# A hybrid encoder block in float32r pairs: the gate stores move to ScalarE's queue, and ScalarE's order in the early feed-forward is written by hand

## The chip, the cores and the metric

One core of a Trainium2 chip runs the whole block. The metric is the device time of one launch in microseconds (us), the median of several runs. Engines: TensorE (PE, with its weight loads PEld), VectorE (DVE), ScalarE (ACT), GpSimd (POOL), and SyncE (SP), which here only issues transfers.

## The reference, cut to what matters

```python
h = concat([meta(16), x(1024)])                     # D = 1024
n = rms_norm(h)
qa, ka, va, qb, kb, vb, ga, gb = split(n @ w_in)
y_a = differential_attention(qa, ka, va)            # 4 heads, two softmaxes each, all keys
y_b = windowed_gqa(qb, kb, vb, sink)                # 8 heads, window 128, sinks
h += (sigmoid(ga) * (y_a @ w_ba) + sigmoid(gb) * (y_b @ w_bb)) @ w_o
f = rms_norm(h)
h += (silu(f @ w_gate) * (f @ w_up)) @ w_down       # D_FF = 2816
out = rms_norm(h)[:, 16:]
```

Everything is float32 at the borders.

## The kernel before, in words

**Precision.** Each factor of a matmul is a pair: a high part (the value rounded to float32r, made by a ScalarE copy, L117 and others) and a low part (the rest, made by a subtraction on VectorE or GpSimd, L118). A product is three matmuls: high by high, high by low, low by high.

**Products of blocks.** The gate projections and the feed-forward are cut into 2 x 2 blocks and computed with seven products instead of eight, numbered 1 to 7, on sums and differences of blocks. Products of one output accumulate in the same PSUM bank: 1, 6, 7 and 4 in one, 2 in another, 5 and 3 in a third. There are eight banks.

**The attention stage** (about 322 to 620 us). A loop over 4 heads x 8 blocks of 128 tokens computes scores (L814), VectorE adds the distance bias and takes the minimum (L817), ScalarE takes the exponential (L824), VectorE combines the two maps (L837), and the block before is transposed (L849) and multiplied with the values (L862). Between these steps `fill` draws single steps from `gate_steps`, the generator of the gate products: a step is three matmuls (L751), and four steps end a product. At the end of products 2, 5, 3 and 4, ScalarE copies the bank into a buffer `gate_stage` (two of them, L759). At the end of 1, 6 and 7, VectorE adds the bank to a buffer `gk` that was loaded from memory (L756). In both cases the result is stored to memory with L760, issued by SyncE; there are 26 stores from `gate_stage` and 24 from `gk`. The next stage loads these results again.

**What sets the order.** TensorE's order is that of the program throughout these stages. The other engines' instructions, and the transfers on SyncE's queue, are ordered by a planner that simulates the program, unless a `manual_schedule` block names the engine: then its instructions keep the program's order. In the first attention block that holds for ScalarE and VectorE.

**The early feed-forward** (about 770 to 836 us). The out projection writes `h` in 128-token blocks; `norm_f` normalises a block (ScalarE's square on L1237), and `turn_f` transposes it into two banks. For blocks 4 to 7, `turn_f` forms sums with the kept halves of blocks 0 to 3 (L1268 to L1274): L1268 and L1272 read the first bank, L1269, L1270 (a ScalarE copy), L1271 (ScalarE, high part) and L1273 the second, so both banks come free when all of these have run, and L1272 needs L1270 first. Block 4 is turned before the loop. The sums are split into pairs for products 6, 5, 7 and 4 by `split_t`: four ScalarE copies (L1321) for each block, GpSimd's low parts for product 4 (L1323), and VectorE's low parts for the others put off to `low_of` (L1325).

The loop over `nf` products (`product_f`, L1347) starts before all blocks are there: for the first three pairs of weight columns (`N_EARLY`) products 1 and 2 come first, since they need only blocks 0 to 3. That is 12 products, with the turns of blocks 5, 6 and 7 ahead of products 0, 2 and 4. `prepare(limit)` makes the weight pairs ahead of use, as many as fit `limit` slots (eight by default): it loads raw weights, forms sums on VectorE for products 6 and 3 (L1163 to L1169), and splits with one ScalarE copy (L117) and one GpSimd subtraction (L118). ScalarE also copies a bank after products 1, 5 and 6 (L1372, L1375) and applies Silu after 2, 7, 3 and 4 (L1358). Before the change only VectorE's order is by hand in products 0 to 11.

Of the kernel before, what the change touches and what calls it, by code (L numbers as in the profile page):

```python
# [9 lines left out]
F32 = mybir.dt.float32  # L10
# [3 lines left out]
AF = mybir.ActivationFunctionType  # L14
# [5 lines left out]
P = 128  # L20
# [53 lines left out]
def encoder_block(ctx: ExitStack, tc: tile.TileContext, x, meta, norm_mix, w_in, lq1, lk1, lq2, lk2,  # L74
                  subln, sink, w_ba, w_bb, w_o, norm_ffn, w_g, w_u, w_d, norm_final, out, dbg=None):
    nc = tc.nc
# [5 lines left out]
    def f32(ap):  # L82
        return ap.bitcast(F32)

    def pool(name, side="left", space=None, bufs=1):
        kw = {} if space is None else {"space": space}
        if space is not DRAM:
            kw["reuse_waits"] = "tile"
        cm = tc.tile_pool(name=name, bufs=bufs, side=side, **kw)
        p = cm.__enter__()  # L90
        return p, lambda: cm.__exit__(None, None, None)

    const, close_const = pool("const")
    small, close_small = pool("small", bufs=4)
# [21 lines left out]
    def split(hi, lo, src, lo_eng):  # L116
        nc.scalar.activation(hi, src, AF.Copy)  # L117
        lo_eng.tensor_tensor(lo, src, f32(hi), ALU.subtract)  # L118
# [41 lines left out]
    def pp_bank(name):  # L160
        return bank(psum1, "pp", name, 3 if psum1 is not psum2 else PP2)
# [304 lines left out]
    for i in range(2):  # L466
        cols = slice(960 * i, 960 * i + 960)
# [37 lines left out]
    def quad(hl, kh, half):  # L505
        return (hT_hi, hT_lo)[hl][:, 4 * kh:4 * kh + 4, half * 512:half * 512 + 512]
# [70 lines left out]
    def load_sums(p, kh, half):  # L577
        for hl in range(2):
            nc.sync.dma_start(f32(quad(hl, kh, half)), ts_d[p][:, hl])
# [35 lines left out]
    def g_place(p, k):  # L615
        row, half = G_OUT[p]
        return g_d[2 * k + row][:, half * 512:half * 512 + 512]
# [23 lines left out]
    def g_ahead(n):  # L641
        for i, (what, far) in enumerate(((g_load, GR_BUFS - 1), (g_split, GO_BUFS - 1))):
            while g_done[i] < min(n + far, len(order_g)):
                if i and held_back is not None:
                    held_back.append(g_done[i])
                else:
                    what(g_done[i])
                g_done[i] += 1
# [74 lines left out]
    for k in range(0, 6, 2):  # L723
        ensure(1)
        wh, wl = prepped.pop((k, k + 1))
        for i in range(2):
# [4 lines left out]
            st = f32(stage.tile([P, 2, 512], F32R, tag="qk", name="gate_first", bufs=QK_BUFS))[:, 0]  # L731
# [10 lines left out]
    def gate_steps():  # L742
        for n, (p, k) in enumerate(order_g):
            g_ahead(n + 1)
            op, act = g_ready.pop((p, k)), G_ACT[p]
            if p in (2, 5, 1):
                g_bank[k] = pp_bank(f"pg{p}_{k}")
            ps = g_bank[k]
            for c in range(4):
                for i, (a, b) in enumerate(((0, 0), (0, 1), (1, 0))):  # L750
                    nc.tensor.matmul(ps, op[:, a, c], quad(b, *act)[:, c], start=(p in (2, 5, 1) and c == 0 and i == 0),  # L751
                                     stop=(p in (2, 3, 4) and c == 3 and i == 2), skip_group_check=True)
                if c == 3:
                    if p in (1, 6, 7):
                        st = g_kept.pop((p, k))
                        nc.vector.tensor_tensor(st, ps, st, ALU.add)  # L756
                    else:
                        st = gpool.tile([P, 512], F32, tag="g", name="gate_stage", bufs=G_BUFS)
                        nc.scalar.copy(st, ps)  # L759
                    nc.sync.dma_start(g_place(p, k), st)  # L760
                    if (p, k) in ((5, 3), (5, 7), (3, 7)):
                        later_p = {(5, 3): 6, (5, 7): 7, (3, 7): 4}[p, k]
                        load_sums(later_p, *G_ACT[later_p])
                yield

    gates = gate_steps()
    close_psum1()
    close_tpool()
# [15 lines left out]
    def branch_w(p, o, src, nme, raw=None):  # L784
        if raw is None:
            raw = raw_tile(f"wbr{nme}_{o}")[:, 0:512]
            load_w(raw, o, src)
        w = raw.rearrange("p (c n) -> p c n", n=P)
        wh = p.tile([P, 2, 4, P], F32R, tag="wh", name=f"wbh{nme}_{o}", bufs=WB_BUFS)
        split(wh[:, 0], wh[:, 1], w, nc.vector if nme == "a" and o >= 4 else nc.gpsimd)  # L790
        return wh
# [208 lines left out]
    def op_tile(name):  # L1000
        return ring.tile([P, 2, 512], F32R, tag="op", name=name, bufs=OP_BUFS)

    def raw_tile(name):
        return ring.tile([P, 1024], F32, tag="raw", name=name, bufs=RING_RAW)
# [3 lines left out]
    def prep_wo(q, c):  # L1008
        w = raw_tile(f"wo_{q}_{c}")[:, 0:512]
        nc.sync.dma_start(w, w_o[c * P:(c + 1) * P, q * 512:q * 512 + 512])  # L1010
        wos[q, c] = op_tile(f"woh_{q}_{c}")
        split(wos[q, c][:, 0], wos[q, c][:, 1], w, nc.gpsimd)
# [4 lines left out]
    for h in range(2):  # L1017
        cols = slice(h * 512, h * 512 + 512)
# [22 lines left out]
    def gated(i, o, half, w, src):  # L1041
        tk = slice(half * 512, half * 512 + 512)
        gt = ypool.tile([P, 512], F32, tag="gt", name=f"gt_{i}_{o}_{half}", bufs=GT_BUFS)
        nc.sync.dma_start(gt, g_d[8 * i + o][:, tk])
        nc.scalar.activation(gt, gt, AF.Sigmoid)
        ps = ps_bank(f"ppa_{o}_{half}_{i}")
        branch_mm(ps, w, src, tk)
        return gt, ps, tk
# [3 lines left out]
    for o in range(DC):  # L1052
        w = first_w[o] if o < 2 else branch_w(ypool, o, w_bb, "b")
        for half in range(2):
            gt, ps, tk = gated(0, o, half, w, yb)
# [16 lines left out]
    for n, (o, half) in enumerate(order_a):  # L1072
        if o not in ws_a:
            ws_a[o] = branch_w(ypool, o, w_ba, "a")
        gt, ps, tk = gated(1, o, half, ws_a[o], ya)
        nc.vector.tensor_tensor(gt, gt, ps, ALU.mult)
        nc.gpsimd.tensor_tensor(gt, gt, tb_row(o, tk), ALU.add)
        split(mT[:, o, 0, tk], mT[:, o, 1, tk], gt, nc.vector)
        if n >= 8:
            prep_wo(0, n - 8)  # L1080
    close_ya()
    close_ya0()
    close_ypool()
# [37 lines left out]
    ops, prepared, used, loaded, freed = {}, [0], [0], [0], [0]  # L1121

    def prepare(limit=OP_BUFS):
        while prepared[0] < len(steps):
            kind, s = steps[prepared[0]]
            need = 1 if kind == "f" else 2
            if used[0] + need > limit or (kind == "d" and prepared[0] >= nf + loaded[0]):
                break
            used[0] += need
            ops[kind, s] = weights(s[2], s[0], s[1]) if kind == "f" else ops_pm(*s)  # L1130
            prepared[0] += 1
        while prepared[0] >= nf and loaded[0] < min(len(steps) - nf, freed[0] + RING_RAW):
            load_d(*steps[nf + loaded[0]][1])
            loaded[0] += 1
# [177 lines left out]
    def c_tile(name):  # L1312
        return cpools[0].tile([P, 512], F32, tag="c", name=name, bufs=C_BUFS) if cpools else p_tile(name)

    lows = {p: [] for p in (6, 5, 7)}

    def split_t(u):
        cols = slice(u * P, u * P + P)
        for p in (6, 5, 7, 4):
            hi, lo, t = t_ops[p][:, 0, :, cols], t_ops[p][:, 1, :, cols], sums_t[u][p]  # L1320
            nc.scalar.activation(hi, t, AF.Copy)  # L1321
            if p == 4:
                nc.gpsimd.tensor_tensor(lo, t, f32(hi), ALU.subtract)  # L1323
            else:
                lows[p].append(lambda hi=hi, lo=lo, t=t: nc.vector.tensor_tensor(lo, t, f32(hi), ALU.subtract))  # L1325

    def low_of(n):
        for p in (6, 5, 7):
            while n > 0 and lows[p]:
                lows[p].pop(0)()  # L1330
                n -= 1

    st = {}
# [64 lines left out]
                nc.sync.dma_start(a_d[3][fp], s4)  # L1398

    AFTER = {0: 5, 2: 6, 4: 7}  # L1400
    for n in range(nf):
        if n not in range(5, 8):
            prepare()
        if n == 0:
            order_dve = tc.manual_schedule(engines={mybir.EngineType.DVE})
            order_dve.__enter__()
        if n in AFTER:
            turn_f(AFTER[n])
            if n == 0:
                split_t(0)  # L1410
            split_t(AFTER[n] - 4)
        product_f(*steps[n][1])
        used[0] -= 1
        if n in (1, 2, 3, 4):
            low_of({1: 1, 2: 1, 3: 1, 4: 1}[n])
        if n == 5:
            prepare(used[0] + 1)
            mults.pop(0)()
            low_of(1)
        if n == 7:  # L1420
            prepare()
            low_of(2)
            mults.pop(0)()
        if n == 9:
            low_of(9)
        if n == 11:
            while mults:
                mults.pop(0)()
            order_dve.__exit__(None, None, None)
            close_h2()  # L1430
            cp, close_cpool = pool("cpool")
            cpools.append(cp)
# [85 lines left out]
    for n in range(nf, len(steps)):  # L1518
        p, j = steps[n][1]
# [3 lines left out]
        if p in LOADS:  # L1523
            at, half, col = LOADS[p]
            if at <= j < at + 4:
                t, cols = 4 * half + j - at, slice(col * 512, col * 512 + 512)
# [60 lines left out]
```

## Time and profile before

| | us |
|---|---|
| median of 3 runs | 1440.44 |
| the runs | 1440.28, 1440.44, 1446.15 |
| the profiled execution | 1441.88 |
| its span, first to last instruction | 1440.0 |
| TensorE busy in the span | 1420.1 |
| ScalarE, VectorE, GpSimd busy | 680.1, 899.8, 643.6 |

The profile lists what each engine did and when. Waits are put down to the instruction or transfer that came last. A group's row gives the line, engine, operation, output <- inputs, shapes and count, then busy time and mean length of one, then the idle time just before, with what ended it. "SPq" is SyncE's queue of transfers, and a transfer's landing is when its data has arrived. The granted TensorE clock is 0.998 over the span.

### The profile page before, as it was taken

The numbers are of one execution on the slowest core, as the hardware profiler recorded it, in microseconds if no ns is written. First come the engines' busy times: TensorE is split into PE (matmuls) and PEld (weight loads), VectorE is DVE, ScalarE is ACT, GpSimd is POOL, SyncE is SP. The second block draws the span as 40 slices with busy tenths as digits, with TensorE's granted clock in tenths as the row PEclk, the third lists the DMA queues.
The fourth block names the chain that finished last, engine by engine and source line by source line (L and its number), as shares of the span: only waits on it lengthen the run. The fifth ranks groups of instructions, "written<-read, shape, count | busy, mean of one in ns | idle before, by whom it ended". The sixth has DMA issues, their size and how long they took to land.

```text
span 1440.0 us, 21175 instructions
## 1 busy us (share of the span) xinstructions
PE 1420.1 (99%) x7279; PEld 1219.3 (85%) x7279; DVE 899.8 (62%) x1624; ACT 680.1 (47%) x1294; POOL 643.6 (45%) x605
## 2 busy tenths in 40 slices
PE   8999999999999999999999999999999999999997
PEld 6988989988888989888888888888888888888886
DVE  7468536637787978624614886555555554787567
ACT  6366535545565656544413743333333333444444
POOL 5599127744433333334622665554454442000444
PEclk9999999999999999999999999999999999999999
DMA  8367668986657464576612535333323333964443
GB/s 246 87 211 235 194 160 275 282 284 221 181 178 257 145 224 141 175 251 207 210 49 88 162 93 176 99 106 105 110 97 101 104 103 102 340 201 142 124 129 139
DMA packets 188891, 242.41 MB, mean 168 GB/s; under 512 B 18208, under 2 KB 115936, under 8 KB 188784
## 3 DMA queue, kind: packets, MB, share of 16 engines
q1 hardware_dynamic: 188784, 241.07, 53.0%
q8 instruction: 57, 0.93, 0.3%
q14 instruction: 50, 0.41, 0.1%
HBM read 157.45 MB, written 77.00 MB: 163 GB/s over the span
## 4 chain that ended last, share of the span: by engine, by line
PE 86%; issue 3%; DMA 3%; POOL 3%; DVE 2%; ACT 2%; SPq 0%; POOLq 0%; ACTq 0%; DVEq 0%
PE pg L1347 28%; PE pd L1462 9%; PE pg L751 7%; PE ppa L796 6%; PE po L1105 6%; PE aps L814 4%; PE pp_ka L214 3%; PE pp_va L214 3%; PE pp_qa L214 3%; PE pp_qb L214 3%; PE apy L862 3%; POOL oa L118 3%; PE apt L849 2%; PE bpt L356 2%; PE bpy L362 2%
## 5 line engine op out<-in xcount | busy, mean ns | idle before, releaser
L118 POOL TENSOR_TENSOR wop<-wf,wop 128x512 fp32r<-128x512 f32 x128 | 172.0, 1348 | 165.5 <-ACT wop L117 153.1
L1347 PE MATMUL pg<-t,wop 128*128 128x512 f32 x1056 | 242.6, 389 | 0.0
L1347 PEld LDWEIGHTS pg<-t,wop 128*128 128x128 f32 x1056 | 198.3, 188 | 41.1
L1462 PE MATMUL pd<-ob,oa 128*128 128x512 f32 x924 | 210.0, 390 | 0.4 <-POOL oa L118 0.4
L1462 PEld LDWEIGHTS pd<-ob,oa 128*128 128x128 f32 x924 | 173.4, 188 | 36.9 <-POOL oa L118 0.8
L1347 PE MATMUL pg<-b,wop 128*128 128x512 f32 x792 | 183.5, 390 | 1.4 <-DVE kept L1272 1.4
L1347 PEld LDWEIGHTS pg<-b,wop 128*128 128x128 f32 x792 | 148.5, 188 | 32.3 <-issue 1.6
L751 PE MATMUL pg<-hT_hi,gop 128*128 128x512 f32 x384 | 142.4, 395 | 0.0
L117 ACT ACTIVATE wop<-wf 128x512 fp32r<-128x512 f32 x128 | 80.3, 632 | 86.9 <-PE pg L1347 47.7
L118 POOL TENSOR_TENSOR oa<-ra,oa 128x512 fp32r<-128x512 f32 x33 | 44.0, 1335 | 170.2 <-ACT oa L117 168.8
L118 POOL TENSOR_TENSOR gop<-gr,gop 128x512 fp32r<-128x512 f32 x47 | 65.5, 1395 | 102.8 <-ACT gop L117 101.7
L117 ACT ACTIVATE oa<-ra 128x512 fp32r<-128x512 f32 x77 | 48.7, 632 | 107.1 <-PE pd L1462 45.8
L824 ACT ACTIVATE as<-as,amn 128x1040 f32<-128x1040 f32 x64 | 74.5, 1164 | 48.6 <-DVE amn L817 37.7
L814 PE MATMUL aps<-ak,aq 128*128 128x392 f32 (+1 forms) x384 | 89.5, 328 | 2.7 <-DVE amn L817 2.1
L1163 DVE TENSOR_TENSOR s<-wf,wf 128x512 f32<-128x512 f32 x22 | 27.3, 1242 | 101.4 <-DMA wf<-in_w_ff_gate_dram 53.2
L1105 PE MATMUL po<-woh,mT 128*128 128x512 f32 x384 | 88.0, 390 | 0.0
L1105 PEld LDWEIGHTS po<-woh,mT 128*128 128x128 f32 x384 | 71.9, 188 | 14.8
L814 PEld LDWEIGHTS aps<-ak,aq 128*128 128x128 f32 x384 | 69.3, 188 | 16.2 <-DVE amn L817 3.3
L751 PEld LDWEIGHTS pg<-hT_hi,gop 128*128 128x128 f32 x384 | 72.3, 188 | 11.2 <-DVE gk L756 0.2
L343 POOL TENSOR_SCALAR bs<-bs,bdn 128x432 f32<-128x432 f32 (+1 forms) x64 | 41.4, 665 | 87.2 <-DVE bdn L341 74.5
L751 PE MATMUL pg<-hT_lo,gop 128*128 128x512 f32 x192 | 75.9, 395 | 0.0
L828 POOL TENSOR_SCALAR as<-as,adn,neglam 128x1040 f32<-128x1040 f32 x32 | 38.9, 1214 | 62.0 <-DVE adn L826 42.6
(292 smaller groups left out, 3101.7 us busy)
## 6 DMA issues: line engine op xcount, KB each, us to landing
ra<-aop SPq DMA_DIRECT2D x77, 256.0 KB, 2.6
wf<-in_w_ff_gate_dram SPq DMA_DIRECT2D x24, 512.0 KB, 3.8
wf<-in_w_ff_up_dram SPq DMA_DIRECT2D x24, 512.0 KB, 3.8
aop<-as SPq DMA_DIRECT2D x44, 256.0 KB, 2.1
w_c<-in_w_in_dram SPq DMA_DIRECT2D x17, 512.0 KB, 6.1
aop<-c SPq DMA_DIRECT2D x33, 256.0 KB, 2.0
ts_d<-to SPq DMA_DIRECT2D x16, 512.0 KB, 3.7
gw<-in_w_in_dram SPq DMA_DIRECT2D x32, 256.0 KB, 4.3
```

The source lines that it names most:

```text
L117: nc.scalar.activation(hi, src, AF.Copy)
L118: lo_eng.tensor_tensor(lo, src, f32(hi), ALU.subtract)
L214: nc.tensor.matmul(ps[:, :n], a[:, c, :], b[:, c, at:at + n], start=(c == 0 and i == 0), stop=(c == DC - 1 and i == 2))
L343: nc.gpsimd.tensor_scalar(st[:, r, :W], st[:, r, :W], dn[:, r:r + 1], 1.0, ALU.mult, ALU.mult)
L751: nc.tensor.matmul(ps, op[:, a, c], quad(b, *act)[:, c], start=(p in (2, 5, 1) and c == 0 and i == 0), stop=(p in (2, 3, 4) and c == 3 and ...
L796: nc.tensor.matmul(ps, w[:, a, j, :], src(j, b, tk), start=(j == 0 and n == 0), stop=(j == 3 and n == 2))
L814: nc.tensor.matmul(ps[:, :n], qs[m][:, t * P:(t + 1) * P], ks[m][:, vv, k0:k0 + n], start=(vv == 0), stop=(vv == 1))
L824: nc.scalar.activation(s[m][:, 0:L], s[m][:, 0:L], AF.Exp, bias=low, scale=-1.0, accum_out=dn[:, m:m + 1])
L862: nc.tensor.matmul(py[:, cols], v[:kp, a, k, :], at_[:kp, k, b, :], start=(k == 0 and j == 0), stop=(k == 8))
L1105: nc.tensor.matmul(ps, mT[:, c, a, t * P:(t + 1) * P], wos[q, c][:, b], start=(c == 0 and n == 0), stop=(c == DC - 1 and n == 2))
L1347: nc.tensor.matmul(ps, op[:, x, c, :], b[:, y, c, :], start=(p in (1, 2, 5) and c == 0 and n == 0), stop=(p in (4, 2, 3) and c == 3 and n ...
L1462: nc.tensor.matmul(ps[u], oa[:, a, u * P:(u + 1) * P], ob[:, b, :], start=(p in (1, 2, 5) and j == 0 and k == 0), stop=(p in (2, 3, 4) and ...
```

## The change

There are three edits, and no matmul is added or removed.

1. The 26 stores from `gate_stage` are issued by ScalarE, right after its copy, and no longer by SyncE. The 24 stores from `gk` stay with SyncE.
2. A Silu of one column is put after the last split of the merged branches, so that ScalarE's function table for Silu is loaded there and not at the first Silu of the feed-forward.
3. In products 0 to 11 of the feed-forward ScalarE's order is by hand too. `split_t`, which made the high copies of a block for all four products at once, becomes `high_t(p, blocks)`, for one product at a time: for product 6 right after the block's turn, for 5, 4 and 7 after products 3 to 8 (`HIGHS`). The weight pairs of products 4 to 7 and 8 to 11 are prepared after the turns of blocks 6 and 7, where before four were prepared ahead of product 0 and one more ahead of each of products 1 to 4.

```diff
-                    nc.sync.dma_start(g_place(p, k), st)
+                    (nc.sync if p in (1, 6, 7) else nc.scalar).dma_start(g_place(p, k), st)
...
+    table = small.tile([P, 1], F32, tag="ss", name="table")
+    nc.scalar.activation(table, gt[:, 0:1], AF.Silu)
...
-    lows = {p: [] for p in (6, 5, 7)}
-
-    def split_t(u):
-        cols = slice(u * P, u * P + P)
-        for p in (6, 5, 7, 4):
+    def high_t(p, *us):
+        for u in us:
+            cols = slice(u * P, u * P + P)
             hi, lo, t = t_ops[p][:, 0, :, cols], t_ops[p][:, 1, :, cols], sums_t[u][p]
             nc.scalar.activation(hi, t, AF.Copy)
             if p == 4:
                 nc.gpsimd.tensor_tensor(lo, t, f32(hi), ALU.subtract)
             else:
                 lows[p].append(lambda hi=hi, lo=lo, t=t: nc.vector.tensor_tensor(lo, t, f32(hi), ALU.subtract))
+
+    lows = {p: [] for p in (6, 5, 7)}
...
     AFTER = {0: 5, 2: 6, 4: 7}
+    HIGHS = {3: ((5, 0),), 4: ((5, 1),), 5: ((5, 2, 3), (4, 0)), 6: ((4, 1, 2),), 7: ((7, 0, 1),), 8: ((7, 2, 3), (4, 3))}
     for n in range(nf):
-        if n not in range(5, 8):
+        if n == 0:
+            order_av = tc.manual_schedule(engines={mybir.EngineType.Activation, mybir.EngineType.DVE})
+            order_av.__enter__()
+        if n > 7:
             prepare()
-        if n == 0:
-            order_dve = tc.manual_schedule(engines={mybir.EngineType.DVE})
-            order_dve.__enter__()
         if n in AFTER:
             turn_f(AFTER[n])
             if n == 0:
-                split_t(0)
-            split_t(AFTER[n] - 4)
+                high_t(6, 0)
+            high_t(6, AFTER[n] - 4)
+            if n:
+                prepare(used[0] + 4)
         product_f(*steps[n][1])
         used[0] -= 1
+        for p, *us in HIGHS.get(n, ()):
+            high_t(p, *us)
         if n in (1, 2, 3, 4):
-            low_of({1: 1, 2: 1, 3: 1, 4: 1}[n])
+            low_of(1)
...
-        if n == 9:
+        if n in (8, 9):
             low_of(9)
         if n == 11:
             while mults:
                 mults.pop(0)()
-            order_dve.__exit__(None, None, None)
+            order_av.__exit__(None, None, None)
```

## The prediction

> **What bounds the kernel now.** I read the page first, then who TensorE waited for, then the chain and the timelines at the places that this gave.
>
> ```profile
> PE 1420.1 (99%) x7279; PEld 1219.3 (85%) x7279; DVE 899.8 (62%) x1624; ACT 680.1 (47%) x1294; POOL 643.6 (45%) x605
> q1 hardware_dynamic: 188784, 241.07, 53.0%
> ```
>
> TensorE is busy for 1420.1 of 1440.0 us, and no edit takes a matmul away, so all that can be won is idle time of TensorE. The second row says that every transfer of the program's own goes through one queue, SyncE's. The waits of TensorE name who holds it up (us in total, times, longest); these are the ones that lie in or after the gated attention stage:
>
> ```profile
> PE aps L814 <- DVE amn L817: 2.1, 5, 0.7
> PE pg L1347 <- DVE kept L1272: 1.4, 1, 1.4
> PE apt L849 <- DVE as L837: 1.1, 2, 1.0
> PE aps L814 <- DMA ak<-ka_d: 0.5, 1, 0.5
> PE apf L883 <- DVE amn L817: 0.3, 1, 0.3
> PE apt L849 <- DVE amn L817: 0.2, 1, 0.2
> ```
>
> One is in the early feed-forward (L1347, 1.4), the other five in the attention stage, 4.2 us together. After the first, the chain of waits is unbroken matmul work for 527 us, so what is won before 814 us reaches the end:
>
> ```profile
> 814.36 408.28 PE pg L1347 x1800
> 1222.64 119.21 PE pd L1462 x526
> ```
>
> **The change part by part.** *The 1.4 us at 814.* TensorE's timeline shows the transposes of block 7, then the gap, then product 4 (counted from 0; a product is 12 matmuls). VectorE's timeline shows why: the subtraction on L1272 of block 6, which frees the bank, itself stood idle for a ScalarE copy.
>
> ```profile
> 811.88 1.04 PE L1253 MATMUL ptn_f<-ident,xn_f 128*128 128x128 f32 x8
> 814.36 22.04 PE L1347 MATMUL pg<-b,wop 128*128 128x512 f32 x96 [1.44 <-DVE kept L1272]
> 808.57 0.68 DVE L1268 TENSOR_TENSOR ts<-ptn_f,kept 128x512 f32<-128x512 f32 x1
> 809.35 0.69 DVE L1269 TENSOR_TENSOR ts<-ptn_f,ts 128x512 f32<-128x512 f32 x1
> 813.52 0.69 DVE L1272 TENSOR_TENSOR kept<-kept,ptn_f 128x512 f32<-128x512 f32 x1 [3.48 <-ACT kept L1270]
> ```
>
> That copy, L1270, could run once L1268 had read the buffer, at 808.57 + 0.68 = 809.25. ScalarE ran it at 812.90, because the planner had put six weight splits (L117) ahead of it, among others:
>
> ```profile
> 808.26 1.15 ACT L117 ACTIVATE wop<-wf 128x512 fp32r<-128x512 f32 x2
> 810.29 1.17 ACT L117 ACTIVATE wop<-wf 128x512 fp32r<-128x512 f32 x2
> 811.86 1.15 ACT L117 ACTIVATE wop<-wf 128x512 fp32r<-128x512 f32 x2
> 812.90 0.58 ACT L1270 COPY kept<-ptn_f 128x512 f32<-128x512 f32 x1
> ```
>
> By hand, L1270 comes right after the transposes' turn: it starts at about 809.25. VectorE goes from L1269 (ends 810.04) straight to L1272 (0.69) and the bank is free at about 810.7. Without the gap product 4 starts when the transposes end, 811.88 + 1.04 = 812.92, so the cover is 2.2 us. **Term 1: -1.4 us.** If the cover fails by x, x of it stays.
>
> What is late next is the weight of product 4. Products 4 to 7 are no longer split at block 5 but behind block 6's copies. On ScalarE L1270, L1271 and the high copy of block 6 take about 0.5 each (back to back, two take 1.15), so the split starts at 809.25 + 1.5 = 810.8 and its high half is done at 811.4; GpSimd needs 1.28 for the low half:
>
> ```profile
> 808.97 2.56 POOL L118 TENSOR_TENSOR wop<-wf,wop 128x512 fp32r<-128x512 f32 x2 [0.87 <-ACT wop L117]
> 806.41 1.70 POOL L1323 TENSOR_TENSOR t<-kept,t 128x512 fp32r<-128x512 f32 x1 [2.58 <-ACT t L1321]
> 806.86 1.79 DVE L1325 TENSOR_TENSOR t<-ts,t 128x512 fp32r<-128x512 f32 x1
> 802.13 0.38 SPq L1144 DMA_DIRECT2D wf<-in_w_ff_gate_dram  x1
> ```
>
> It is ready at 812.7, and the low half is first used by the third matmul of product 4, after 812.9: a thin cover of 0.2 to 0.6 us. It gets about 1.1 us thicker because GpSimd's p = 4 low (L1323 at 806.41) moves to product 5 and later, and VectorE's L1325, which took 1.79 beside it where L1268 takes 0.68 for as many elements, no longer delays L1268. The raw weight is issued at 802.13 and was there for the split at 808.26. Products 5 to 7 then gain: a product lasts 22.04 / 8 = 2.75 us, a low half 1.28. Products 8 to 11, split behind block 7, have two more products of cover. VectorE's lows of p = 5 and 7 are wanted at products 14 and 16 and come one product earlier than now. I cost all this at nothing.
>
> *The Silu table.* Its load is 1.28 us at 816.60 on ScalarE; it moves into a hole of 15 us. TensorE does not wait for it now, nor does VectorE, so it is worth 0; if ScalarE's hole were filled it would cost 1.3 of ScalarE and still nothing of TensorE.
>
> ```profile
> 816.60 1.28 ACT L1358 ACT_TABLE_LOAD   x1
> 732.35 0.63 ACT L117 ACTIVATE woh<-wo 128x512 fp32r<-128x512 f32 x1 [14.97 <-PE po L1105]
> ```
>
> *The 26 gate stores.* The copies of products 2, 5, 3 and 4 (L759) go through two buffers; each waits until the store before last has landed. Twice that wait held ScalarE, 8.1 us together (first row; then the tile's own view, SyncE's timeline and, with 10.03, the chain):
>
> ```profile
> ACT gate_stage L759 <- DMA g_d<-gate_stage: 8.1, 2, 5.2
> L759 ACT COPY gate_stage<-pg x26: 561/586/598, 328.5 to 621.0; 128x512 f32<-128x512 f32 x26
> L760 SPq DMA_DIRECT2D g_d<-gate_stage x26: 319/320/806, 329.3 to 621.7; - x26
> DMA to landing us min/median/max: 2.0/4.4/10.2
> 379.06 1.21 SPq L666 DMA_DIRECT2D ak<-ka_d  x2
> 385.75 10.03 DMA g_d<-gate_stage
> 385.75 0.32 SPq L760 DMA_DIRECT2D g_d<-gate_stage  x1
> ```
>
> A store takes 2.0 us alone and 10 when it stands behind large loads: the one of 385.75 follows the key loads of the next head from 379.06 on. Behind the held copy stood the exponentials, behind those VectorE and the banks of the scores. The waits of TensorE in the stretches 340 to 352 and 393 to 402 us:
>
> ```profile
> PE aps L814 <- DVE amn L817: 1.0, 2, 0.7
> PE apt L849 <- DVE as L837: 0.2, 1, 0.2
> PE aps L814 <- DVE amn L817: 0.4, 1, 0.4
> ```
>
> With the 0.5 for the key load and the 0.2 of L849 on L817 (both in the second stretch) that is 2.3 us. The key load belongs here because SyncE stood at a store for a copy while the loads queued up behind it:
>
> ```profile
> 378.17 0.36 SPq L760 DMA_DIRECT2D g_d<-gate_stage  x1
> 378.59 0.42 SPq L664 DMA_DIRECT2D ak<-ka_d  x1
> ```
>
> On a queue of its own the store does not stand behind the loads that SyncE issued earlier, and SyncE no longer waits for copies. No row shows two queues side by side: between 0 and 2.3 us go. I take all of it, since a landing of even 6 us instead of 10 would free the copy before the exponential asks. **Term 2: -2.3 us.** On this the Trainium skill has a rule each way. "DMA: Bandwidth & Descriptors", Queues, rings and completion order, says that a DMA engine takes packets in turn from the queues that have work, which is what I forecast. The same page, under Issuing engines are not separate DMA queues, says that issuing from several engines saves only issue time; by that the landing would stay and term 2 be near 0.
>
> What ScalarE pays: today its next instruction starts some 0.5 us after a copy's start; now it must see the copy end (0.586) and issue (0.32), so about 0.45 us more each, 26 x 0.45 = 11.7 us. Behind it queue exponentials, transposed copies and gate splits. ScalarE has room, and its exponentials mostly wait for VectorE anyway (a stretch, the copies in it, the exponentials of the whole):
>
> ```profile
> 322.00:400.00 78.00, 75.14 (x431) 65.64 (x431) 56.84 (x165) 46.49 (x88) 32.94 (x25) 1.00 0.62 203
> L759 ACT COPY gate_stage<-pg x13: 561/587/598, 328.5 to 397.5; 128x512 f32<-128x512 f32 x13
> L824 ACT ACTIVATE as<-as,amn 128x1040 f32<-128x1040 f32 x64 | 74.5, 1164 | 48.6 <-DVE amn L817 37.7 <-DVE as L838 8.9 <-POOL gop L118 1.4
> ```
>
> ScalarE (fourth engine) is busy 46.5 of 78 us where 13 of the 26 stores lie. Bounds: 0 and 11.7; I take 0.3, near the lower end, because of these 31.5 idle us against 13 x 0.45 = 5.9: less than one store's price reaches TensorE. **Term 3: +0.3 us.** The planner will also order SyncE, VectorE and GpSimd of that stage anew; I put that at 0 with about 1 us either way.
>
> Sum: -1.4 - 2.3 + 0.3 = -3.4 us. The profiled execution took 1441.88 us (span 1440.0 and 1.88 around it), so a profile would show about 1438.5. That execution is 1.4 above the median of the runs, 1440.44; against the median the forecast is **1437.0 us**.
>
> **The rivals.**
> *The stores land no sooner* (they share the engines with the same loads). Only term 1 stays: 1440.4 - 1.4 = 1439.0. For it: 0.62 of the DMA engines' time was taken in that stretch. Against: 10 us for what takes 2 alone looks like standing in line.
> *The split a block later becomes the new wait.* If ScalarE or the raw weight is 1 to 1.5 us later than I count, product 4 waits for GpSimd's low half, a price of one half (1.28): 1437.0 + 1.3 = 1438.3. For it: the cover is the thinnest of all.
> *Slower: ScalarE as the store's issuer holds the attention stage.* Place: a store ahead of an exponential that VectorE is ready for. Price 0.45 each. From 3.7 / 0.45 = 8 of 26 on it outweighs terms 1 and 2; with half of them, and no earlier landing, 1440.4 - 1.4 + 5.9 = 1444.9; with all, 1450.7. Against: the 48.6 us that exponentials stand idle for.
> *More goes:* the other attention waits, 4.2 - 2.3 = 1.9 us, vanish with the new order too: 1435.1.
> *The hand order changes nothing* because the bank waits for something else as well: then -2.0 alone, 1438.4. The 3.48 us that L1272 waited speak against it.
>
> **How the numbers follow.** Forecast 0.50; stores no sooner 0.17; split late 0.11; ScalarE holds attention 0.10; more goes 0.08; hand order idle 0.04. The range 1434.3 to 1442.0 takes in the forecast with the planner's microsecond, the rivals near it, and the slower one up to six stores passed through with no earlier landing (1439.0 + 6 x 0.45 = 1441.7); left out are the rest of that rival and lucky re-plans. Half a per cent, about what a measurement of this kernel can tell from no change, is 7.2 us. Faster by that needs all 5.6 us of the waits above and more (0.03); slower, 1447.6, needs 19 or more of 26 stores on the path with no earlier landing (0.04); within it 0.93.
>
> **What would show it.** Right: no wait of L1347 near 813 and L1272 of block 6 running at once behind L1269; a table load near 717; a second hardware queue on the page with 26 stores; stores landing in 2 to 5 us; no wait of the L759 copy for a store. Wrong: stores still at 8 to 10 us, TensorE waits for exponentials' users at new places between 340 and 600 us, or product 4 waiting for GpSimd.

## The result, and the profile after

The changed kernel takes 1447.14 us (median of 10 runs, 1443.96 to 1449.5) and the kernel before, on the same chip in the same session, 1442.06 (10 runs, 1439.14 to 1446.15). The ratio is 1.0033 with a 95% interval of 1.0021 to 1.0045: a loss of 0.33%, inside the half per cent that the prediction called no change, but with the wrong sign and above the range's upper end of 1442.0. The profiled execution is the slowest of the ten: 1449.5 us, with a span of 1447.7 and a granted clock of 0.995 over it (before: 1441.88, 1440.0 and 0.998).

From the page of the changed kernel, the engines' busy time and the new hardware queue:

```profile
PE 1424.2 (98%) x7279; PEld 1222.2 (84%) x7279; DVE 908.1 (63%) x1624; ACT 680.6 (47%) x1295; POOL 650.6 (45%) x605
q10 hardware_dynamic: 3744, 6.82, 1.2%
```

The 26 stores have a queue of their own, as planned. TensorE runs the same 7279 instructions, yet is busy 4.1 us longer: some of its matmuls became slower. VectorE gained 8.3 us, also with the same count of instructions. The waits of TensorE in the feed-forward and in the attention stage (us in total, times, longest) say where its idle time is now:

```profile
PE pg L1349 <- DVE c L1358: 4.7, 1, 4.7
PE aps L814 <- DVE amn L817: 1.0, 3, 0.5
PE apt L849 <- DVE amn L817: 0.9, 1, 0.9
PE apt L849 <- DVE as L837: 0.7, 1, 0.7
PE aps L814 <- DMA ak<-ka_d: 0.7, 1, 0.7
```

The 1.4 us for the block's turn is gone from the feed-forward, and a single wait of 4.7 us stands there instead, for an addition. (Lines behind about 1080 are two higher than before: L1347 is now L1349, L1356 is L1358, L1361 is L1363; L1325 is the same.) The attention stage has 4.0 us where it had 4.2 (three more rows of 0.2 to 0.3 are not shown). TensorE's timeline around the early feed-forward:

```profile
813.57 1.04 PE L1255 MATMUL ptn_f<-ident,xn_f 128*128 128x128 f32 x8
814.36 22.05 PE L1349 MATMUL pg<-b,wop 128*128 128x512 f32 x96
836.25 5.60 PE L1349 MATMUL pg<-t,wop 128*128 128x512 f32 x24
846.59 13.80 PE L1349 MATMUL pg<-t,wop 128*128 128x512 f32 x48 [4.74 <-DVE c L1358]
```

Product 4 follows the transposes without a gap. Eight products later (96 matmuls), and after two more (24), product 14 stands still until 846.59, and its first matmuls are slow: 48 take 13.80 us, where at the rate of the row of 96 they take 48 x 22.05 / 96 = 11.0. Both kernels start product 4 at 814.36, by chance. Before, the 72 matmuls of products 12 to 17 ran from 836.23 to 852.71:

```profile
836.23 16.48 PE L1347 MATMUL pg<-t,wop 128*128 128x512 f32 x72
```

After, the same 72 end at 846.59 + 13.80 = 860.39, 7.7 us later: 4.7 of gap, 2.8 of slow matmuls, the rest rounding where rows overlap. That is as much as the spans differ, but not the edits' net effect. The first and last starts in the tiles' views (the numbers around "to") divide the span. Before, then after: the scores of the attention stage, the first early product and the last matmul of the gate and up products.

```profile
L814 PE MATMUL aps<-ak,aq x384: 275/340/447, 325.5 to 585.5; 128*128 128x392 f32 x128, 128*128 128x256 f32 x64
L1347 PE MATMUL pg<-b,wop x792: 387/389/476, 800.0 to 1216.8; 128*128 128x512 f32 x198
L1347 PE MATMUL pg<-t,wop x1056: 388/389/390, 836.2 to 1222.2; 128*128 128x512 f32 x176
```

```profile
L814 PE MATMUL aps<-ak,aq x384: 275/340/448, 327.6 to 587.1; 128*128 128x392 f32 x128, 128*128 128x256 f32 x64
L1349 PE MATMUL pg<-b,wop x792: 387/389/476, 801.7 to 1224.5; 128*128 128x512 f32 x198
L1349 PE MATMUL pg<-t,wop x1056: 388/389/763, 836.3 to 1229.9; 128*128 128x512 f32 x176
```

Ahead of 325.5, where nothing was edited, this profile lost 2.1 us by chance: from 26 to 30 us its granted clock was 0.55 to 0.59, where the profile before shows 1.00. The attention stage went from 260.0 to 259.5 and the feed-forward from 1222.2 - 800.0 = 422.2 to 1229.9 - 801.7 = 428.2: +6.0, which is the +7.7 behind product 4 less 1.7 won ahead of it (814.36 - 800.0 = 14.4 us before, 814.36 - 801.7 = 12.7 after). The medians differ by 5.1. The longest matmul of the last row, 763 ns where 390 was the longest, is one of the slow ones.

VectorE's timeline says what the addition L1358 stood behind, in the kernel after (eight rows) and before (three):

```profile
811.34 0.69 DVE L1274 TENSOR_TENSOR kept<-kept,ptn_f 128x512 f32<-128x512 f32 x1 [0.71 <-ACT kept L1272]
...
836.10 1.79 DVE L1366 TENSOR_TENSOR c<-c,p 128x512 f32<-128x512 f32 x1
837.81 1.78 DVE L1325 TENSOR_TENSOR t<-ts,t 128x512 fp32r<-128x512 f32 x1
839.52 3.46 DVE L1325 TENSOR_TENSOR t<-kept,t 128x512 fp32r<-128x512 f32 x2
842.90 1.74 DVE L1171 TENSOR_TENSOR wf<-wf,wf 128x512 f32<-128x512 f32 x1
844.57 1.28 DVE L1325 TENSOR_TENSOR t<-kept,t 128x512 fp32r<-128x512 f32 x2
845.77 0.68 DVE L1358 TENSOR_TENSOR c<-pg,p 128x512 f32<-128x512 f32 x1
```

```profile
836.48 0.68 DVE L1356 TENSOR_TENSOR c<-pg,p 128x512 f32<-128x512 f32 x1
837.08 1.18 DVE L1325 TENSOR_TENSOR t<-ts,t 128x512 fp32r<-128x512 f32 x1
838.18 4.68 DVE L1325 TENSOR_TENSOR t<-kept,t 128x512 fp32r<-128x512 f32 x4
```

This addition takes product 9's result out of its bank, and that bank is product 14's. Before, it ran at 836.48 and five subtractions (the last low of p = 5 and the four of p = 7, `low_of(9)`) came behind it. After, the five stand ahead of it, since `low_of(9)` is called after product 8 as well and VectorE's order is by hand. And the first three are slow: 1.7 to 1.8 us each until 843, where one takes 0.64 in the pair at 844.57, which ran while GpSimd was idle (from 844.10 to 847.71). So two suspects: **theory A**, the five lows a product early; **theory B**, VectorE's work slowed because GpSimd works beside it. GpSimd's timeline after, with one of VectorE's rows from the same time, and GpSimd's p = 4 lows in the view of their tile (ns min/median/max, first and last start), after and then before:

```profile
812.93 6.12 POOL L118 TENSOR_TENSOR wop<-wf,wop 128x512 fp32r<-128x512 f32 x4 [7.41 <-ACT wop L117]
820.33 6.57 POOL L118 TENSOR_TENSOR wop<-wf,wop 128x512 fp32r<-128x512 f32 x4 [1.29 <-ACT wop L117]
822.33 0.69 DVE L1358 TENSOR_TENSOR c<-pg,p 128x512 f32<-128x512 f32 x1
```

```profile
L1323 POOL TENSOR_TENSOR t<-kept,t x4: 1722/1734/1744, 826.9 to 840.7; 128x512 fp32r<-128x512 f32 x4
```

```profile
L1323 POOL TENSOR_TENSOR t<-kept,t x4: 1288/1304/1695, 806.4 to 824.2; 128x512 fp32r<-128x512 f32 x4
```

GpSimd stood idle for 7.41 us while no weight was split, and did that work, and the p = 4 lows, later: the lows started from 826.9 to 840.7 instead of 806.4 to 824.2, and took 1.73 us each instead of 1.30. The stretch 822 to 842 us by engine, which is the same work in both, since both start product 4 at 814.36 (us; then busy time and instructions of PE, PEld, DVE, ACT and POOL; clock, DMA share, GB/s), before and after:

```profile
822.00:842.00 20.00, 20.00 (x90) 16.57 (x89) 19.75 (x22) 7.55 (x14) 12.11 (x8) 1.00 0.17 54
```

```profile
822.00:842.00 20.00, 19.85 (x88) 16.12 (x86) 19.75 (x17) 10.45 (x20) 17.93 (x11) 1.00 0.27 85
```

VectorE was full in both, 19.75 of 20 us. Before, it did 22 instructions in that time, after 17; GpSimd's busy time rose from 12.1 to 17.9. VectorE had no slack here, so each slowed instruction pushed everything behind it in the hand order.

On this the Trainium skill, "SBUF — State Buffer", Who interferes with whom, says that a VectorE instruction with two SBUF inputs and a GpSimd instruction that reads SBUF exclude each other, and that one with at most one SBUF input does not contend. The trace agrees: L1325, with both inputs in SBUF, goes from 0.64 to about 1.75 us, GpSimd's L1323 from 1.30 to 1.73, and L1358, which reads a bank, takes 0.69 at 822.33 in the midst of GpSimd's four splits, and 0.68 at 845.77, where GpSimd is idle.

### The profile page after: what moved, and what is told of

Its sections match the earlier page's. It is cut to its first block, busy times and chain, and to the rows that moved or that the text cites. A ratio compares the mean times of both kernels' runs of the same rounds, so it can differ in the third digit from the quotient of the medians.

```text
span 1447.7 us, 21172 instructions
## 1 busy us (share of the span) xinstructions
PE 1424.2 (98%) x7279; PEld 1222.2 (84%) x7279; DVE 908.1 (63%) x1624; ACT 680.6 (47%) x1295; POOL 650.6 (45%) x605
## 5 line engine op out<-in xcount | busy, mean ns | idle before, releaser
L1349 PE MATMUL pg<-t,wop 128*128 128x512 f32 x1056 | 245.5, 392 | 4.7 <-DVE c L1358 4.7
L1349 PEld LDWEIGHTS pg<-t,wop 128*128 128x128 f32 x1056 | 200.0, 190 | 47.0 <-issue 5.1
L1349 PE MATMUL pg<-b,wop 128*128 128x512 f32 x792 | 183.5, 389 | 0.0
L1349 PEld LDWEIGHTS pg<-b,wop 128*128 128x128 f32 x792 | 148.4, 188 | 30.7
L1165 DVE TENSOR_TENSOR s<-wf,wf 128x512 f32<-128x512 f32 x22 | 25.3, 1150 | 100.2 <-DMA wf<-in_w_ff_up_dram 50.8
```

The source lines that it names most:

```text
L1165: tt(s1, a21, a22, ALU.add)
L1349: nc.tensor.matmul(ps, op[:, x, c, :], b[:, y, c, :], start=(p in (1, 2, 5) and c == 0 and n == 0), stop=(p in (4, 2, 3) and c == 3 and n ...
```

## The experiments

**The parts of the change.** The kernel before with edit 1 alone (the stores), and the changed kernel without edits 1 and 2 (edit 3 alone):

> The kernel before with only the 26 gate stores moved to ScalarE's queue. As forecast (stores land sooner, cost on ScalarE small): 2.0 us under the kernel before, the waits of TensorE in the attention stage 4.2 us down to about 2. Rival (stores land no sooner): within 0.5 us of the kernel before, waits near 4 us, median landing still 4 to 5 us.

> The changed kernel without the other two edits: stores with SyncE, Silu's table loaded at the first Silu, ScalarE by hand in the early feed-forward. Theory A or B: the wait at product 14 is there as in the changed kernel (4.7 us and about 2.8 us of slow matmuls behind it), the 1.4 us wait at product 4 is gone, in sum 6 us above the kernel before. If the Silu load at the first Silu matters, ScalarE is 1.3 us later there and the wait grows by up to that. If instead the moved stores caused the loss, this run is 1.5 us under the kernel before.

These two and the next two ran on one chip with one set of runs of the kernel before (29, median 1442.34). Stores alone: 1441.28 (12 runs), ratio 0.9994 (0.9984 to 1.0004); TensorE's waits in the attention stage came to 5.0 us there and not to 2, with 2.3 of it for one key load. Edit 3 alone: 1447.53 (6 runs), 1.0042 (1.0026 to 1.0058), with the wait of the changed kernel to the tenth:

```profile
PE pg L1347 <- DVE c L1356: 4.7, 1, 4.7
```

The whole loss is in the feed-forward's new order, and the stores' gain is between nothing and 0.16%.

**Undoing A: the five lows back after product 9.**

```diff
-        if n in (8, 9):
+        if n == 9:
             low_of(9)
```

> The changed kernel with one line put back: the remaining low parts of products 5 and 7 (five L1325 on VectorE) are issued after product 9 only, not after product 8. Theory A (the five low parts stand in VectorE's hand order ahead of the addition of product 9 that frees the bank for product 14): the addition starts near 839.5 us, product 14 does not wait (4.74 us before), no slow clock follows, and the time falls by 6.5 to 7.7 us against the changed kernel, to 1 to 2 us under the kernel before. The price may be up to 1 us at product 16, which then gets its low parts late. Theory B (VectorE is slow because GpSimd's low parts of product 4 now run beside it): at least 3 us of wait at product 14 stay, and the time is 3 us or more above the kernel before.

1444.79 (12 runs, 1440.67 to 1447.96), ratio 1.0018 (1.0005 to 1.0031). Product 14 no longer waits, but product 15 does, for the bank that the next result's copy-out frees:

```profile
PE pg L1349 <- DVE p L1363: 3.7, 1, 3.7
```

The five lows stand ahead of that one (L1363) now. A alone is not the cause: from the turn of block 7 to this copy-out VectorE's order is that of the kernel before, row by row, and the kernel before waits for nothing. But VectorE is late:

```profile
835.93 0.68 DVE L1358 TENSOR_TENSOR c<-pg,p 128x512 f32<-128x512 f32 x1
```

This addition runs 3.2 us behind the start of product 12 (832.7 in this profile), where before it ran 0.3 us behind it (836.48 and 836.2). So some 3 us were lost before the five lows began, with no change of VectorE's order; GpSimd was busy for 17.9 of the 20 us up to 5.8 us behind the start of product 12, as in the changed kernel.

**Undoing B in part: GpSimd's p = 4 lows, and the high copies that go with them, after product 11.**

```diff
-    HIGHS = {3: ((5, 0),), 4: ((5, 1),), 5: ((5, 2, 3), (4, 0)), 6: ((4, 1, 2),), 7: ((7, 0, 1),), 8: ((7, 2, 3), (4, 3))}
+    HIGHS = {3: ((5, 0),), 4: ((5, 1),), 5: ((5, 2, 3),), 7: ((7, 0, 1),), 8: ((7, 2, 3),), 11: ((4, 0, 1, 2, 3),)}
```

> The changed kernel with the high copies and GpSimd low parts of product 4 (four L1323) put off to product 11; the five VectorE low parts stay ahead of product 9's addition. Theory A: VectorE still has seven operations ahead of the addition; GpSimd's weight splits still run beside some of them, so 2 to 4 us of the wait stay and the time is 1 to 4 us above the kernel before. Theory B: VectorE's operations take 0.7 instead of 1.7 us from 824 to 842 us, the addition starts before 841.8 us, product 14 does not wait, and the time is 1 to 2 us under the kernel before.

1442.37 (12 runs), 1.0008 (0.9997 to 1.0019). Product 14's wait fell from 4.7 to 0.6 with the five lows still ahead of the addition; another of 2.0 came at product 20:

```profile
PE pg L1349 <- DVE c L1358: 2.6, 2, 2.0
```

```profile
818.10:838.10 20.00, 19.76 (x88) 16.02 (x86) 19.73 (x21) 8.28 (x16) 13.04 (x8) 1.00 0.29 84
855.69 0.69 DVE L1165 TENSOR_TENSOR s<-wf,wf 128x512 f32<-128x512 f32 x1 [6.22 <-DMA wf<-in_w_ff_up_dram]
```

The second row is the same work as 822 to 842 in the changed kernel: this profile starts product 12 at 832.3 and not 836.3, so 20 us are taken up to 5.8 us behind that start. GpSimd is down to 13.0 us, and VectorE did 21 instructions in 19.73 us where it had done 17 in 19.75. B is real: with less work on GpSimd beside it VectorE gets more done. The third row is the cause of the wait at product 20: the addition for it stands behind a sum of weights (L1165) that waits for its load, and the chain of waits leads from that load back to a weight split of GpSimd at 850.62, which had queued behind the four moved lows (842.51 to 848.92).

**Undoing the rest of B: weight splits two ahead after product 1, so that GpSimd is not idle.**

```diff
-                prepare(used[0] + 4)
+                prepare(min(OP_BUFS, used[0] + 4))
         product_f(*steps[n][1])
         used[0] -= 1
+        if n == 1:
+            prepare(used[0] + 2)
```

> The changed kernel with the weight splits of products 4 and 5 put after product 1 and those of 6 to 9 behind block 6's copies, so that GpSimd, idle for 7.4 us before 812.9 us in the changed kernel, begins about 4 us earlier; the five low parts stay ahead of product 9's addition. Theory B (GpSimd's work was pushed to where VectorE is full, and each slows the other): VectorE's operations between 820 and 842 us take less than the 1.7 us of now, the wait at product 14 falls from 4.74 us to under 1.5, no slow clock follows, and the time is 5 to 7 us under the changed kernel. Theory A (the order on VectorE alone): 3 us or more of the wait stay.

**Undoing A more gently: one low after product 8, two after 9, the rest after 11.**

```diff
-        if n in (8, 9):
-            low_of(9)
+        if n in (8, 9, 11):
+            low_of({8: 1, 9: 2, 11: 9}[n])
```

> The changed kernel with VectorE's low parts spread: one after product 8, two after product 9, two after product 11, behind the additions that free banks. Theory A alone: no wait at products 14 to 16, 1 to 2 us under the kernel before. Theory A and B together (VectorE is simply late beside GpSimd): the order no longer costs anything at product 14, but 1 to 2 us of waits stay at products 15 and 16, and the time is within 1 us of the kernel before.

**Both of these.**

> Both: GpSimd earlier and VectorE's low parts spread. If A and B together are the whole cause, TensorE waits less than 0.5 us in all between 812 and 870 us, the 1.4 us wait at product 4 stays gone, and the time is 1.5 to 2 us under the kernel before and 6 to 8 us under the changed kernel. If something else is short (ScalarE by hand, the raw weights), a wait of 1 us or more shows at another product.

The three ran on one chip with one set of runs of the kernel before (27, median 1442.37). The early splits alone: 1443.29 (11 runs), 1.0006 (0.9997 to 1.0016). The spread lows alone: 1442.17 (11), 0.9998 (0.9989 to 1.0007). Both: 1439.36 (11), 0.9983 (0.9974 to 0.9992). The remaining waits, in that order:

```profile
PE pg L1349 <- DVE c L1358: 2.8, 1, 2.8
```

```profile
PE pg L1349 <- DVE p L1363: 2.0, 1, 2.0
```

```profile
PE pg L1349 <- DVE p L1363: 0.5, 1, 0.5
```

The wait of the early splits alone (2.8) is more than I expected. Of the 4.7 us the first edit takes off 1.9, the second 2.7 (its wait is at product 15), and both leave 0.5. GpSimd's idle time ahead of the weight splits went from 7.41 to 3.73 us in the version with both:

```profile
804.81 2.54 POOL L118 TENSOR_TENSOR wop<-wf,wop 128x512 fp32r<-128x512 f32 x2 [3.73 <-ACT wop L117]
```

In the 20 us up to 5.8 us behind the start of product 12, GpSimd was busy for 16.2 us with the early splits alone and with both, against 17.9, so they thin out its work there only in part.

The tiles' views of the version with both say where its gain lies:

```profile
L814 PE MATMUL aps<-ak,aq x384: 275/340/452, 325.8 to 582.4; 128*128 128x392 f32 x128, 128*128 128x256 f32 x64
L1349 PE MATMUL pg<-b,wop x792: 387/389/476, 797.2 to 1213.3; 128*128 128x512 f32 x198
L1349 PE MATMUL pg<-t,wop x1056: 387/389/495, 831.8 to 1218.7; 128*128 128x512 f32 x176
```

The feed-forward takes 421.5 us, 6.7 less than in the changed kernel and 0.7 less than before: of the 1.4 us of idle time won at product 4, half is kept. The attention stage takes 256.6 instead of 260.0, more than in the changed kernel (259.5), though the stores are the same in both. That length scatters from profile to profile: in the ten profiles with the stores on ScalarE it was 255.6 to 261.3, 258.0 on average, and in the three with them on SyncE 260.0, 260.1 and 258.5.

**That version again, and two variants of it on the same chip** (kernel before: 27 runs, median 1441.86): the same again, the same with the 26 stores back on SyncE, and the same with GpSimd's p = 4 lows after products 9 to 11.

> The kernel with early splits and spread low parts once more, beside the two that follow: 2 to 3.5 us under the kernel before, one wait of about 0.5 us of TensorE in the early feed-forward.

> The kernel with early splits and spread low parts, its 26 gate stores issued by SyncE again. If the stores' queue is worth nothing (median landing 4.4 against 4.8 us, waits of the attention stage 4.2 against 4.0): within 1 us of the run with ScalarE's stores. If moving them is worth what was forecast: 2 us above it.

> The kernel with early splits and spread low parts, and GpSimd's four low parts of product 4 put off to products 9 to 11. If the two engines' mutual slowing is what is left: GpSimd's busy time from 822 to 842 us falls from 16.6 to under 13 us, VectorE's operations there number 20 or more instead of 18, the last 0.5 us of wait is gone, and the time falls by up to 0.7 us. Rival: the low parts come too late for product 20, or its neighbour's additions do, and 1 to 2 us of wait appear near 857 us, as when they were put off to product 11 alone.

Again: 1439.22 (11 runs), 0.9979 (0.9968 to 0.9990). Stores on SyncE: 1440.18 (11), 0.9987 (0.9977 to 0.9996). Later p = 4 lows: 1439.7 (11), 0.9984 (0.9975 to 0.9993). In all three profiles the feed-forward takes 421.5 to 421.7 us. So the order with both repairs beats the kernel before, by 0.1 to 0.2%, and the changed kernel, with or without the moved stores. With the stores on SyncE the medians are 1.7 us apart, more than the 0.7 that the feed-forward shows; the interval (0.6 to 3.3 us) holds both. Moving GpSimd's lows on top brings nothing more that can be told apart. It did thin out GpSimd's work, from 16.2 to 13.7 us in the 20 us up to 5.8 us behind product 12's start, and VectorE did 23 instructions there instead of 19. But the wait only moved, from 0.55 at 842 to 0.84 at 853, ahead of product 20, where the addition again came behind a weight's sum that had waited for its load (3.23 us):

```profile
853.45 8.93 PE L1349 MATMUL pg<-t,wop 128*128 128x512 f32 x38 [0.84 <-DVE c L1358]
```

**The slow matmuls.** To see whether the gap itself makes them slow, I put 100 small matmuls of zeros (48x48) behind product 13, added to its bank.

> The changed kernel with 100 small matmuls of zeros after product 13, added into its open bank, so that TensorE is not idle for the whole 4.74 us ahead of product 14; nothing else is moved. Theory (the idle stretch lowers the granted clock, and the matmuls behind it run at half speed for some 6 us): product 14 starts as late as in the changed kernel, within 0.3 us, but its matmuls follow each other by 0.229 us and not by 0.427, and the time is 2.5 to 2.8 us under the changed kernel. Rival (the slow matmuls come from what runs beside them, memory traffic or the other engines): they stay slow, and the time is that of the changed kernel.

1451.89 (5 runs), 1.0063 (1.0050 to 1.0075), and no answer: the filling had to wait itself, for ScalarE's copy out of that bank, and made the gap 8.8 us.

```profile
848.16 4.16 PE L1422 MATMUL pg<-pad 128*48 128x48 bf16 x100 [8.83 <-ACT u L1379]
```

It shows one thing beside: the slow matmuls were now the filling, with a granted clock of 0.50 from 848.2 to 852.2, and product 14 behind it ran at full rate, at 1.00. The granted clock in the kernels that waited is the better witness. First the changed kernel from 847 and from 853, behind its gap of 4.74 us; then one row each of the spread lows (gap 2.05 us by the timeline), the early splits (2.83) and the five lows after product 9 (3.66), all taken within about 1 us behind the gap:

```profile
847.00:853.00 6.00, 6.00 (x17) 4.61 (x17) 3.56 (x5) 4.75 (x10) 5.29 (x4) 0.56 0.66 178
853.00:860.00 7.00, 7.00 (x32) 5.79 (x31) 5.89 (x6) 1.11 (x2) 3.62 (x3) 1.00 0.60 184
```

```profile
844.20:847.20 3.00, 3.00 (x9) 2.33 (x8) 3.00 (x3) 2.02 (x5) 3.00 (x3) 0.51 0.95 325
```

```profile
842.30:845.50 3.20, 3.12 (x8) 2.52 (x9) 1.92 (x3) 3.20 (x7) 2.01 (x2) 0.53 0.40 107
```

```profile
844.60:850.00 5.40, 5.36 (x24) 4.42 (x24) 2.68 (x3) 3.10 (x7) 5.23 (x4) 1.00 0.78 243
```

In the first row 17 matmuls took 6 us, in the second 32 took 7. The clock (the third number from the end) was near half for some microseconds after gaps of 4.74, 2.05 and 2.83 us, and 1.00 after one of 3.66; it was 1.00 too after the gap of 2.03 us at product 20 in the kernel with GpSimd's p = 4 lows after product 11. The matmuls were slow where the granted clock was near half and at their usual rate where it was 1.00; what length of gap brings it down these rows do not settle. The kernel of the last row has run times that fit: its three runs with a clock of 0.999 over the span, the profiled one among them, took 1440.7 to 1442.2 us, its two at 0.998 took 1444.4 and 1445.0, and its seven at 0.995 to 0.997 took 1443.9 to 1448.0.

## Why the prediction was wrong

**Wrong at one step, "I cost all this at nothing".** The prediction saw that the lows of p = 5 and 7 come one product earlier, and asked only when they are wanted, at products 14 and 16. It did not ask what they now stand in front of. VectorE's order is by hand, so the five lows of `low_of(9)` held the addition that frees product 14's bank. The step also counted the moved p = 4 lows and weight splits as a gain for GpSimd's cover at product 4 and never as a load in the stretch to which they go. The prediction even had the price in hand: it quotes an L1325 of 1.79 us beside GpSimd against 0.68 for as many elements, and used it for the one row that the move relieves. In place of nothing the profile shows +7.7 us at product 14, and the experiments show that it takes both causes: repairs of one alone leave 2.0 to 3.7 us of wait in all, repairs of both together 0.5.

**No row asked whether VectorE had slack.** The view of 822 to 842 us was there in the profile before: 19.75 of 20 us busy, though 62% over the span. The list of rivals had a late split, a held ScalarE and an idle hand order, but none that begins at VectorE, the engine whose order the edit changes.

**Term 1 was right in mechanism and size.** L1274 (before, L1272) runs with a wait of 0.71 instead of 3.48, product 4 follows the transposes, and 1.4 us of idle time went (forecast -1.4). The thin cover of the weight of product 4 held: no wait for GpSimd there.

**Term 2 was mis-sized: -2.3 was taken.** The stores from their own queue (view of the tile, from issue to landing), and ScalarE's remaining wait for one:

```profile
L760 ACTq DMA_DIRECT2D g_d<-gate_stage x26: 326/326/356, 329.8 to 624.0; - x26
  DMA g_d<-gate_stage: 3.0, 1
DMA to landing us min/median/max: 2.0/4.8/7.7
```

The median landing went from 4.4 to 4.8, only the longest fell, from 10.2 to 7.7, and the held copies cost 3.0 us instead of 8.1. It is the same in every profile: with the stores on SyncE the median is 4.1 to 4.4 and the longest 10.2 to 10.4, with them on ScalarE 4.8 to 5.2 and 7.4 to 9.3. What that gave TensorE has three measures, none of them sharp: 1442.34 - 1441.28 = 1.1 us by the medians with the stores alone, 1440.18 - 1439.22 = 1.0 by taking them off the repaired version (both with overlapping intervals), and 259.5 - 258.0 = 1.5 between the averages of the stage's length, which scatters by more. So terms 2 and 3 together are worth about 1 us instead of 2.0, between the forecast and the rival by which the stores land no sooner. Of the two rules that the prediction weighed, that of the Trainium skill, "DMA: Bandwidth & Descriptors", Issuing engines are not separate DMA queues, fits the median landing, which did not improve; the shorter maximum and the small gain leave room for the other.

**The table was right, and nothing speaks against term 3.** No wait of TensorE in the attention stage names ScalarE; what the 26 issues cost there was not measured by itself. The table load is off the path, in a hole of 14.69 us of ScalarE:

```profile
717.86 1.28 ACT L1082 ACT_TABLE_LOAD   x1
```

**What stays open.** How the 4.7 us divide between the two causes is not settled, since they multiply (more lows, each longer). The larger share seems to be the load from GpSimd: with VectorE's order as before 3.7 us of wait stay, and with the lows early but GpSimd's p = 4 lows elsewhere product 14 waits 0.6. The record does not show either why a gap of 3.66 us left the clock up once, or why TensorE's wait for a key load was 0.5, 0.7 and 2.3 us in the profiles before, after and of the stores alone.

## What to carry to other kernels

When an edit moves an instruction in an order written by hand, look at what it now stands ahead of: on that engine the next instruction that frees a bank is the deadline, not the use of the moved result. Before work is moved into a stretch, read that stretch's windows: an engine at 62% over the span was at 99% just there. And count work moved on GpSimd against VectorE's subtractions that read SBUF twice, by the longest row of such a pair that the profile has.

## What the runs showed of the hardware that was not expected

A gap of TensorE can cost more than its length: behind the 4.74 us, matmuls came 0.43 us apart instead of 0.23 for some microseconds (granted clock 0.56), which added 2.8 us. The Trainium skill, "TensorE: Matmul & The Clock Gate", What's actually happening, says that the clock falls to half after an idle window of about 3.4 us, on a window that runs freely. The half rate agrees. The length does not quite: half clock followed gaps of 2.05 and 2.83 us, and none followed one of 2.03 and one of 3.66 us. Early in the changed kernel's profile it came too, from 26 to 30 us (0.55 to 0.59), where no wait of TensorE had been longer than 1.8 us.

VectorE and GpSimd slow each other by a lot and not evenly: a subtraction of 128x512 took 0.64 to 0.68 us on VectorE alone and 1.7 to 1.8 beside GpSimd, while GpSimd's went from 1.30 to 1.73.
